# Eight-product and seven-product units in the second SwiGLU: five of eight units in seven products, with two of the weight sums formed in HBM

## The chip, the cores and the metric

The kernel runs on one core of one Trainium2 chip. The metric is device time in microseconds (us) of one execution. TensorE (PE) multiplies, VectorE (DVE) and ScalarE (ACT) work on vectors, GpSimd (POOL) and SyncE (SP) here mostly start DMA transfers. The kernel before took 1850.46 us in the median of three runs (1849.84 to 1851.51).

## The reference

One residual block on 16 meta tokens and 256 tokens of width 2048, all in float32:

```python
h = h + 0.5 * swiglu(rmsnorm(h, ffn1_norm), ffn1_w_gate, ffn1_w_up, ffn1_w_down)
u = rmsnorm(h, mix_norm);  z = u @ w_in
# z -> pooling channels | q | k | v | forget logits: pooled means and causal attention
h = h + mix @ w_out
h = h + 0.5 * swiglu(rmsnorm(h, ffn2_norm), ffn2_w_gate, ffn2_w_up, ffn2_w_down)
return h[:, N_META:]
# swiglu(x, wg, wu, wd) = (silu(x @ wg) * (x @ wu)) @ wd;  D_FF = 5632
```

Nearly all of the time goes into streaming 330 MB of weights through matrix products: the first SwiGLU, the input projection and attention, the output projection, and the second SwiGLU, in that order.

## The kernel before, in words

**Split products.** A float32 operand is split into a rounded part `hi` (ScalarE, L199) and a remainder `lo` (VectorE, L201), and a product is three matmuls: hi*hi, hi*lo, lo*hi. Each weight load `raw` is [128 x 1024] floats (512 KB), goes into one of six `raw` buffers, and is split into one of four `hi` and four `lo` buffers.

**One list for the whole kernel.** `W(...)` and `C(...)` append weight steps and other steps to `items`; `run` (L212 on) walks the list. It issues loads ahead (`do_dma`), splits up to `ahead` steps ahead, and lets `fn` multiply. All loads go through SyncE's queue, one after the other. The compiler's scheduler then orders the instructions of each engine, and may put one that waits for nothing ahead of others that were written earlier.

**First SwiGLU** (about 44 to 760 us). Every 512 KB load feeds 24 matmuls of 272 columns.

**Second SwiGLU** (from about 1124 us). It is tiled in 17 groups: 11 gate-up groups `f2_j` and 6 down groups `d2_tm` (thirds of 4, 4 and 3 gate-up groups, two halves each). A group runs over units (8 each; the last two down groups have 6), and a unit is a 2x2 block product. Kind "P" does it in eight products: two weight loads, two splits, 24 matmuls of 512 columns. Kind "S" does it in seven (Strassen-like): 21 matmuls, with four weight steps, since sums of weight blocks are operands too. `kinds` (L717) picks units 2, 4 and 6 as S, the last one always P. `PLAN` (L847) says which operand each product takes, and at which of the steps.

**An S unit before.** Step 0 splits only one half of the first load (512 columns, L886 to L890). Step 1 splits the second load; VectorE forms `T0` with two adds of 512 (L901, L902). Step 2 splits `T0`, and VectorE forms `T1` with two more adds (L907, L908). Step 3 splits `T1`. So VectorE does, per S unit, one half split, three whole splits and four half adds; per P unit two whole splits. The activation side (`operands`, L720) builds four sums per S unit and two per P unit, once for each unit.

**Around the groups.** `evac` functions combine the seven accumulators in PSUM on VectorE and ScalarE; `tokens_off` (L1027) transposes the gate-up results and calls `operands`, within units 2 and 3 of the next group.

GpSimd does nothing between its start and 805 us; then it clears two tiles and issues 20 small transfers for attention (L415, L466).

Of the kernel before, what the change touches and what calls it, by code (L numbers as in the profile page):

```python
# [8 lines left out]
F32 = mybir.dt.float32  # L9
# [3 lines left out]
ALU = mybir.AluOpType  # L13
# [22 lines left out]
def hymba_block(ctx: ExitStack, tc: tile.TileContext, t, out: bass.AP):  # L36
# [11 lines left out]
    lop = ctx.enter_context(tc.tile_pool(name="lop", bufs=4))  # L48
    hsp = ctx.enter_context(tc.tile_pool(name="hsp", bufs=1, side="right"))
# [106 lines left out]

    def W(src, nk, fn, split=None, ahead=2):
        items.append(("w", src, nk, fn, split or split_w, ahead))
# [53 lines left out]
    def run(items):  # L212
# [9 lines left out]
        def do_dma():  # L222
            n = st["d"]
            _, src, nk, _, _, _ = items[ws[n]]
            if n % 4 == 0 and n < 4 * len(FIRST):
                load_h(*FIRST[n // 4])
# [12 lines left out]
        for kind, _, _, fn, _, ahead in items:  # L239
# [5 lines left out]
            while st["s"] < min(n + 1 + ahead, len(ws)):  # L245
                do_split()
# [470 lines left out]
    def kinds(n):  # L717
        return ["S" if i in (2, 4, 6) and i < n - 1 else "P" for i in range(n)]
# [65 lines left out]
    def out_evac(d):  # L784
        def f():
# [6 lines left out]
            else:  # L792
                sq = x3p.tile([P, SEQ], F32, tag="sq2", name=f"sq_n2{d}")
# [36 lines left out]
    def finish2():  # L830

        f2 = later_pools["f2"]
        v, y, s = (f2.tile([P, 2], F32, tag=f"n{i}", name=f"n2_{i}") for i in range(3))
# [18 lines left out]
    def halfcols(x):  # L852
        return x.rearrange("p a n -> p (a n)").rearrange("p (m c) -> p m c", m=2)

    def group(name, side, src, evac, between):
# [23 lines left out]
        for u, kd in enumerate(units):  # L879
            raw = {}  # L880

            def first_block(r, n, raw=raw):
                raw[0] = halfcols(r)
# [3 lines left out]
                nc.scalar.copy(hi[:, 0], raw[0][:, 0])  # L887
                nc.vector.tensor_tensor(
                    out=lo[:, 0], in0=raw[0][:, 0], in1=hi[:, 0].bitcast(F32), op=ALU.subtract
                )  # L890
                return hi, lo

            def sums(r, n, raw=raw, i=0):

                def tile_(k):
                    return later_pools["f2"].tile([P, HALF, P], F32, tag=f"T{k}", name=f"{name}T{k}_{n}")
                if i == 0:
                    raw[1] = halfcols(r)
                    raw["T0"] = tile_(0)
                    T = halfcols(raw["T0"])  # L900
                    nc.vector.tensor_add(T[:, 0], raw[0][:, 0], raw[0][:, 1])  # L901
                    nc.vector.tensor_add(T[:, 1], raw[0][:, 1], raw[1][:, 1])  # L902
                    return split_w(r, n)
                if i == 1:
                    raw["T1"] = tile_(1)
# [230 lines left out]
```

## Time and profile before

| | |
|---|---|
| median of three runs | 1850.46 us (1849.84 to 1851.51) |
| profiled execution | 1850.18 us |
| its span, first to last instruction | 1848.4 us |
| TensorE busy | 1839.9 us, 11,718 matmuls |
| VectorE busy | 1348.7 us, 73% of the span |
| ScalarE busy | 969.5 us, 52% |
| DMA | 335.56 MB, mean 182 GB/s |
| mean granted TensorE clock | 1.000 |

The profile is one execution. Busy time of TensorE is the union of its matmul rows, which overlap: a matmul row of 512 columns lasts some 396 ns, but the next starts earlier, so what a matmul costs is read from the distance of starts. The same is true, less strongly, of VectorE. The DMA share is the mean busy share of the core's 16 DMA engines. A wait is put down to what ended it last.

### The profile page before, as it was taken

To read this page: it belongs to the slowest core of one execution; us is meant where nothing else is said; L and a number is where in the kernel's file an instruction comes from. 1 tells how busy PE (TensorE), PEld (TensorE's weight loads), DVE (VectorE), ACT (ScalarE), POOL (GpSimd) and SP (SyncE) were. 2 spreads that over 40 slices of the span, in tenths; PEclk is the share of its full clock that TensorE was granted. 3 is DMA by queue.
4 is the path that set the end of the run, shared out by engine and by line. 5 is a ranking of instruction groups with operands and counts; after the bars stand their busy time and mean duration, and the time that the engine had idled before them with its cause. 6 is when DMAs were issued, how large, how long until landed. Compare 5 with 4: busy or idle time off the path is not lost.

```text
span 1848.4 us, 29522 instructions
## 1 busy us (share of the span) xinstructions
PE 1839.9 (100%) x11718; PEld 1679.0 (91%) x11718; DVE 1348.7 (73%) x1848; ACT 969.5 (52%) x1302; POOL 12.4 (1%) x32
## 2 busy tenths in 40 slices
PE   9999999999999999999999999999999999999998
PEld 8999999999999999999999988888888888888887
DVE  7655544555544555678777878888998999988988
ACT  7434333444334343577675566666655555555563
POOL 0000000000000000002000000000000000000000
PEclk9999999999999999999999999999999999999999
DMA  8555555555555554565445555555666555656654
GB/s 287 172 171 171 176 178 172 173 176 174 174 173 177 176 171 153 171 201 161 142 156 160 182 188 179 197 189 182 194 200 201 191 190 191 193 192 204 201 186 137
DMA packets 96825, 335.56 MB, mean 182 GB/s; under 512 B 11424, under 2 KB 13488, under 8 KB 96688
## 3 DMA queue, kind: packets, MB, share of 16 engines
q1 hardware_dynamic: 96048, 333.65, 55.1%
q8 instruction: 91, 1.49, 0.3%
q14 instruction: 46, 0.38, 0.1%
q0 software_dynamic: 640, 0.04, 0.0%
HBM read 331.51 MB, written 2.10 MB: 180 GB/s over the span
## 4 chain that ended last, share of the span: by engine, by line
PE 95%; DVE 2%; ACT 1%; issue 1%; DMA 0%; SPq 0%; ACTq 0%; DVEq 0%
PE f1d L170 5%; PE f1u L171 5%; PE f1g L171 5%; PE f1g L172 5%; PE f1d L172 5%; PE f1d L171 5%; PE f1g L170 5%; PE f1u L170 5%; PE f1u L172 5%; PE wo L176 3%; PE z L170 2%; PE z L172 2%; PE z L171 2%; PE wo L180 2%; PE z L176 1%; DVE lo L201 1%
## 5 line engine op out<-in xcount | busy, mean ns | idle before, releaser
L199 ACT CAST hi<-raw 128x1024 fp32r<-128x1024 f32 (+2 forms) x601 | 609.4, 1016 | 638.5 <-PE f1g L171 144.3
L201 DVE TENSOR_TENSOR lo<-raw,hi 128x1024 fp32r<-128x1024 f32 (+2 forms) x601 | 708.1, 1180 | 322.0 <-ACT hi L199 318.9
L170 PE MATMUL f1g<-x,hi 128*128 128x272 f32 x704 | 203.9, 290 | 1.7 <-ACT hi L199 1.7
L172 PE MATMUL f1g<-x,lo 128*128 128x272 f32 x704 | 203.9, 290 | 0.3 <-DVE lo L201 0.2
L171 PE MATMUL f1u<-x,hi 128*128 128x272 f32 x704 | 203.8, 289 | 0.0
L171 PE MATMUL f1g<-x,hi 128*128 128x272 f32 x704 | 203.7, 289 | 0.0
L172 PE MATMUL f1u<-x,lo 128*128 128x272 f32 x704 | 203.6, 289 | 0.0
L170 PE MATMUL f1u<-x,hi 128*128 128x272 f32 x704 | 203.5, 289 | 0.0
L172 PE MATMUL f1d<-f1s,lo 128*128 128x272 f32 x704 | 203.1, 289 | 0.0
L170 PE MATMUL f1d<-f1s,hi 128*128 128x272 f32 x704 | 203.1, 288 | 0.0
L171 PE MATMUL f1d<-f1s,hi 128*128 128x272 f32 x704 | 202.8, 288 | 0.0
L170 PEld LDWEIGHTS f1g<-x,hi 128*128 128x128 f32 x704 | 132.3, 188 | 2.6 <-ACT hi L199 2.4
L172 PEld LDWEIGHTS f1g<-x,lo 128*128 128x128 f32 x704 | 133.3, 189 | 0.8 <-DVE lo L201 0.7
L171 PEld LDWEIGHTS f1d<-f1s,hi 128*128 128x128 f32 x704 | 133.9, 190 | 0.0
L172 PEld LDWEIGHTS f1u<-x,lo 128*128 128x128 f32 x704 | 133.4, 189 | 0.0
L171 PEld LDWEIGHTS f1g<-x,hi 128*128 128x128 f32 x704 | 132.6, 188 | 0.0
L171 PEld LDWEIGHTS f1u<-x,hi 128*128 128x128 f32 x704 | 132.6, 188 | 0.0
L170 PEld LDWEIGHTS f1u<-x,hi 128*128 128x128 f32 x704 | 132.3, 188 | 0.0
L170 PEld LDWEIGHTS f1d<-f1s,hi 128*128 128x128 f32 x704 | 132.3, 188 | 0.0
L172 PEld LDWEIGHTS f1d<-f1s,lo 128*128 128x128 f32 x704 | 132.3, 188 | 0.0
L170 PE MATMUL z<-x,hi 128*128 128x272 f32 (+3 forms) x384 | 111.3, 290 | 0.0
L172 PE MATMUL z<-x,lo 128*128 128x272 f32 (+3 forms) x384 | 110.4, 287 | 0.1
(780 smaller groups left out, 3771.5 us busy)
## 6 DMA issues: line engine op xcount, KB each, us to landing
raw<-in_wgu SPq DMA_DIRECT2D x344, 512.0 KB, 3.5
raw<-in_wd SPq DMA_DIRECT2D x168, 512.0 KB, 3.4
raw<-in_win SPq DMA_DIRECT2D x66, 512.0 KB, 3.5
raw<-in_wout SPq DMA_DIRECT2D x32, 512.0 KB, 4.3
raw<-in_wd SPq DMA_DIRECT2D x16, 256.0 KB, 3.3
raw<-in_wgu SPq DMA_DIRECT2D x16, 128.0 KB, 3.3
raw<-in_wgu SPq DMA_DIRECT2D x8, 256.0 KB, 5.4
out<-h SPq DMA_DIRECT2D x8, 256.0 KB, 3.3
```

Source lines behind the costliest of these rows:

```text
L170: nc.tensor.matmul(ps[:, :n], wh, x[:, 0, :], start=first, stop=False)
L171: nc.tensor.matmul(ps[:, :n], wh, x[:, 1, :], start=False, stop=False)
L172: nc.tensor.matmul(ps[:, :n], wl, x[:, 0, :], start=False, stop=last)
L176: nc.tensor.matmul(ps.rearrange("p (a n) -> p a n", a=2), wh, x, start=first, stop=last)
L180: nc.tensor.matmul(ps[:, SEQ:], wl, x[:, 0, :], start=False, stop=False)
L199: nc.scalar.copy(hi, raw)
L201: nc.vector.tensor_tensor(out=lo, in0=raw, in1=hi.bitcast(F32), op=ALU.subtract)
```

## The change

`kinds` now makes units 2 to 6 seven-product units: five of eight instead of three (in the last two down groups, with 6 units, three instead of two). The former `T0` is no longer added up on VectorE. Instead, `add_up` makes a [128 x 1024] tile in HBM for each S unit: two plain transfers on SyncE's queue copy the same half of the first weight block into both halves of the tile, HBM to HBM, 256 KB each with rows of 2 KB; two transfers on GpSimd's queue then add the two other halves to it (`accum_op=ALU.add`), 256 KB each. Step 2 loads that tile like a weight. `T1` stays on VectorE, as one tile `T`. Step 0 loads only the half that it splits.

The jobs of `add_up` are collected in the list `ahead`; `do_dma` is written to take one off every ninth step from step 20 on. There are 81 S units in place of 49 (55 of gate-up, 26 of down), so 81 jobs: 162 copies and 162 accumulating transfers.

To make room in SBUF, the scratch `sq` of the output projection and the small tiles of `finish2` use the buffer `t2`, which `operands` uses too.

```diff
...
     rawp = ctx.enter_context(tc.tile_pool(name="rawp", bufs=6))
     hip = ctx.enter_context(tc.tile_pool(name="hip", bufs=4))
     lop = ctx.enter_context(tc.tile_pool(name="lop", bufs=4))
+    dram = ctx.enter_context(tc.tile_pool(name="dram", bufs=1, space=bass.MemoryType.DRAM))
     hsp = ctx.enter_context(tc.tile_pool(name="hsp", bufs=1, side="right"))
 
     first_x, first_g, first_t = (ctx.enter_context(ExitStack()) for _ in range(3))
...
 
 
     items = []
+
+
+    ahead, AHEAD_EVERY = [], 9
 
     def W(src, nk, fn, split=None, ahead=2):
         items.append(("w", src, nk, fn, split or split_w, ahead))
...
         def do_dma():
             n = st["d"]
             _, src, nk, _, _, _ = items[ws[n]]
+            if n >= 20 and n % AHEAD_EVERY == 0 and ahead:
+                ahead.pop(0)()
+            if callable(src):
+                src = src()
             if n % 4 == 0 and n < 4 * len(FIRST):
                 load_h(*FIRST[n // 4])
             if src is not None:
...
             st["s"] += 1
 
         n = 0
-        for kind, _, _, fn, _, ahead in items:
+        for kind, _, _, fn, _, more in items:
             while st["d"] < len(ws) and loads[st["d"]] - loads[n] <= DMA_AHEAD:
                 do_dma()
             if kind == "c":
                 fn()
                 continue
-            while st["s"] < min(n + 1 + ahead, len(ws)):
+            while st["s"] < min(n + 1 + more, len(ws)):
                 do_split()
             fn(splits.pop(n))
             n = min(n + 1, len(ws) - 1)
...
 
 
     def kinds(n):
-        return ["S" if i in (2, 4, 6) and i < n - 1 else "P" for i in range(n)]
+        return ["S" if i in (2, 3, 4, 5, 6) and i < n - 1 else "P" for i in range(n)]
 
     def operands(src, kind, base, ext, name):
 
...
                 f2n["acc"] = x3p.tile([P, SEQ], F32, tag="acc2", name="acc_n2")
                 nc.scalar.activation(f2n["acc"], h[d][:, META:], AF.Square)
             else:
-                sq = x3p.tile([P, SEQ], F32, tag="sq2", name=f"sq_n2{d}")
+                sq = x3p.tile([P, SEQ], F32, tag="t2", name=f"sq_n2{d}")
                 nc.scalar.activation(sq, h[d][:, META:], AF.Square)
                 nc.vector.tensor_add(f2n["acc"], f2n["acc"], sq)
             u = d // 2
...
 
     def finish2():
 
-        f2 = later_pools["f2"]
-        v, y, s = (f2.tile([P, 2], F32, tag=f"n{i}", name=f"n2_{i}") for i in range(3))
+        n2 = later_pools["x3p"].tile([P, 6], F32, tag="t2", name="n2_t")
+        v, y, s = (n2[:, 2 * i : 2 * i + 2] for i in range(3))
         for i in range(2):
             ps = ps_q(f"ps_n2{i}")[:, :2]
             nc.tensor.matmul(
...
     def halfcols(x):
         return x.rearrange("p a n -> p (a n)").rearrange("p (m c) -> p m c", m=2)
 
+    def add_up(name, b1, b2):
+
+        got = {}
+
+        def job():
+            x = got[0] = dram.tile([P, HALF, P], F32, tag=f"sum{name}", name=f"sum{name}")
+            for m in range(2):
+                nc.sync.dma_start(out=x[:, 4 * m : 4 * m + 4, :], in_=b1[:, 4:, :])
+            for m, b in enumerate((b1[:, :4, :], b2[:, 4:, :])):
+                nc.gpsimd.dma_start(out=x[:, 4 * m : 4 * m + 4, :], in_=b, accum_op=ALU.add)
+
+        ahead.append(job)
+        return lambda: got[0]
+
     def group(name, side, src, evac, between):
 
 
...
             raw = {}
 
             def first_block(r, n, raw=raw):
-                raw[0] = halfcols(r)
+                raw[0] = r
                 hi, lo = (
                     later_pools["f2"].tile([P, 1, NB], F32R, tag=f"b{i}", name=f"{name}b{i}_{n}") for i in range(2)
                 )
-                nc.scalar.copy(hi[:, 0], raw[0][:, 0])
-                nc.vector.tensor_tensor(
-                    out=lo[:, 0], in0=raw[0][:, 0], in1=hi[:, 0].bitcast(F32), op=ALU.subtract
-                )
+                r = r.rearrange("p a n -> p (a n)")
+                nc.scalar.copy(hi[:, 0], r)
+                nc.vector.tensor_tensor(out=lo[:, 0], in0=r, in1=hi[:, 0].bitcast(F32), op=ALU.subtract)
                 return hi, lo
 
-            def sums(r, n, raw=raw, i=0):
-
-                def tile_(k):
-                    return later_pools["f2"].tile([P, HALF, P], F32, tag=f"T{k}", name=f"{name}T{k}_{n}")
-                if i == 0:
-                    raw[1] = halfcols(r)
-                    raw["T0"] = tile_(0)
-                    T = halfcols(raw["T0"])
-                    nc.vector.tensor_add(T[:, 0], raw[0][:, 0], raw[0][:, 1])
-                    nc.vector.tensor_add(T[:, 1], raw[0][:, 1], raw[1][:, 1])
-                    return split_w(r, n)
-                if i == 1:
-                    raw["T1"] = tile_(1)
-                    T = halfcols(raw["T1"])
-                    nc.vector.tensor_add(T[:, 0], halfcols(raw["T0"])[:, 1], raw[0][:, 0])
-                    nc.vector.tensor_add(T[:, 1], T[:, 0], raw[1][:, 0])
-                    return split_w(raw["T0"], n)
-                return split_w(raw["T1"], n)
+            def second(r, n, raw=raw):
+                raw[1] = r
+                return split_w(r, n)
+
+            def third_(r, n, raw=raw):
+                raw["T"] = later_pools["f2"].tile([P, HALF, P], F32, tag="T", name=f"{name}T{n}")
+                T = raw["T"]
+                nc.vector.tensor_add(T[:, :4], r[:, 4:], raw[0])
+                nc.vector.tensor_add(T[:, 4:], T[:, :4], raw[1][:, :4])
+                return split_w(r, n)
+
+            def fourth(r, n, raw=raw):
+                return split_w(raw["T"], n)
 
             steps = range(2) if kd == "P" else range(4)
             for st in steps:
...
                     for n, pr in enumerate(PLAN[kd]):
                         if pr[2] == st:
                             product(u, n, hl)
-                split = None
-                if kd == "S":
-                    split = first_block if st == 0 else (
-                        lambda r, n, f=sums, i=st - 1: f(r, n, i=i)
-                    )
-                W(src(u, st) if st < 2 else None, HALF, mul, split, ahead=3)
+                if kd == "P":
+                    W(src(u, st), HALF, mul, None, ahead=3)
+                elif st == 0:
+                    W(src(u, 0)[:, :4, :], 4, mul, first_block, ahead=3)
+                elif st == 1:
+                    W(src(u, 1), HALF, mul, second, ahead=3)
+                elif st == 2:
+                    W(add_up(f"{name}_{u}", src(u, 0), src(u, 1)), HALF, mul, third_, ahead=3)
+                else:
+                    W(None, HALF, mul, fourth, ahead=3)
             for fn in between.get(u, ()):
                 C(fn)
 
```

What the scheduler makes of it is seen in the order of the instructions. The first place is SyncE's queue early in the first SwiGLU; `raw` are weight loads, `sumf2_1_2` is the sum tile for unit 2 of gate-up group 1. Before:

```order
L229 DMA raw36_846<-in_wgu1 128x1024
L229 DMA raw37_876<-in_wgu1 128x1024
L229 DMA raw38_917<-in_wgu1 128x1024
L229 DMA raw39_947<-in_wgu1 128x1024
L229 DMA raw40_977<-in_wgu1 128x1024
```

Now, at the same loads:

```order
L870 DMA sumf2_0_5_1458<-in_wgu2 128x512 x2
L237 DMA raw40_989<-in_wgu1 128x1024
L870 DMA sumf2_0_6_1755<-in_wgu2 128x512 x2
L237 DMA raw41_1019<-in_wgu1 128x1024
L870 DMA sumf2_1_2_2052<-in_wgu2 128x512 x2
L237 DMA raw42_1060<-in_wgu1 128x1024
L870 DMA sumf2_1_3_2349<-in_wgu2 128x512 x2
L237 DMA raw43_1090<-in_wgu1 128x1024
```

The copies do not stand at every ninth step. They wait for nothing, and stand between neighbouring loads: one or two after each load. The first two copies stand behind load 27, the next two behind load 36, and all 162 are issued before load 127 (of some 730); behind that there are none.

The second place is the end of the accumulating transfers on GpSimd's queue, and what follows (`d2_21` is the last group of all, `one2` and `nil` are the two tiles cleared for attention):

```order
L872 DMA sumd2_21_2_18225<-in_wd2 128x512 x2
L872 DMA sumd2_21_3_18364<-in_wd2 128x512 x2
L872 DMA sumd2_21_4_18505<-in_wd2 128x512 x2
L407 MEMSET one2_9352 128x272
L408 MEMSET nil_9353 128x272
L423 DMA cuq0_9543<-c0_9531 1x16x16
```

All 162 accumulating transfers stand in front of GpSimd's work for attention, which stood right behind its start-up before.

The third place is VectorE in a gate-up group, with two S units in a row now (`f2_5` is group 5; `f2_5b1` is the half split, `lo` a whole split, `f2_5T` an add of 512):

```order
L901 TENSOR_TENSOR f2_5T0_559_15704<-raw558_15625 128x512
L201 TENSOR_TENSOR lo555_15665<-f2_5T1_554_15627,hi555_15663 128x1024
L902 TENSOR_TENSOR f2_5T0_559_15704<-raw558_15625,raw559_15646 128x512
L907 TENSOR_TENSOR f2_5T1_560_15725<-f2_5T0_559_15704,raw558_15625 128x512
L201 TENSOR_TENSOR lo556_15674<-raw556_15555,hi556_15672 128x1024
L734 TENSOR_TENSOR sg1_15659<-ga1_15655 128x256
L725 TENSOR_TENSOR gb1_15653<-ga1_15655,gb1_15653 128x512
L888 TENSOR_TENSOR f2_5b1_558_15693<-raw558_15625,f2_5b0_558_15692 128x512
L201 TENSOR_TENSOR lo557_15684<-raw557_15589,hi557_15682 128x1024
L736 TENSOR_TENSOR ge1_15654<-sg1_15659,ge1_15654 128x256
L201 TENSOR_TENSOR lo559_15709<-raw559_15646,hi559_15707 128x1024
L908 TENSOR_TENSOR f2_5T1_560_15725<-f2_5T1_560_15725,raw559_15646 128x512
```

and now:

```order
L911 TENSOR_TENSOR f2_5b1_586_16121<-raw586_16057,f2_5b0_586_16120 128x512
L744 TENSOR_TENSOR ge1_16102<-sg1_16107,ge1_16102 128x256
L205 TENSOR_TENSOR lo585_16113<-f2_5T584_16081,hi585_16111 128x1024
L205 TENSOR_TENSOR lo587_16134<-raw587_16069,hi587_16132 128x1024
L921 TENSOR_TENSOR f2_5T588_16142<-raw588_16094,raw586_16057 128x512
L205 TENSOR_TENSOR lo588_16147<-raw588_16094,hi588_16145 128x1024
L922 TENSOR_TENSOR f2_5T588_16142<-f2_5T588_16142,raw587_16069 128x512
L911 TENSOR_TENSOR f2_5b1_590_16172<-raw590_16118,f2_5b0_590_16171 128x512
L205 TENSOR_TENSOR lo589_16159<-f2_5T588_16142,hi589_16157 128x1024
L205 TENSOR_TENSOR lo591_16185<-raw591_16130,hi591_16183 128x1024
L921 TENSOR_TENSOR f2_5T592_16193<-raw592_16155,raw590_16118 128x512
```

Of four adds per S unit two are left, and S units follow each other without a P unit between them.

## Rows read from the trace of the kernel before

**Rows 1.** Page, part 1: busy time, share of the span, instructions of two engines

```profile
PE 1839.9 (100%) x11718; PEld 1679.0 (91%) x11718; DVE 1348.7 (73%) x1848; ACT 969.5 (52%) x1302; POOL 12.4 (1%) x32
```

**Rows 2.** Page, part 2: granted clock and DMA share, in tenths, 40 slices

```profile
PEclk9999999999999999999999999999999999999999
DMA  8555555555555554565445555555666555656654
```

**Rows 3.** Page, part 4: the chain that ended last, by engine

```profile
PE 95%; DVE 2%; ACT 1%; issue 1%; DMA 0%; SPq 0%; ACTq 0%; DVEq 0%
```

**Rows 4.** Stages: busy time (and instructions) of each engine, clock, DMA share, GB/s

```profile
core 0: us, PE busy (x) PEld busy (x) DVE busy (x) ACT busy (x) POOL busy (x), PEclk, DMA share, GB/s
15.00:20.00 5.00, 4.07 (x31) 3.62 (x29) 3.78 (x11) 3.75 (x10) 0.00 (x0) 1.00 0.99 331
46.00:370.00 324.00, 324.00 (x2567) 324.00 (x2567) 173.69 (x211) 129.11 (x151) 0.00 (x0) 1.00 0.53 173
1124.00:1848.00 724.00, 719.71 (x3148) 580.46 (x3147) 649.94 (x814) 416.04 (x481) 0.00 (x0) 1.00 0.58 189
1430.90:1474.50 43.60, 43.60 (x193) 35.19 (x192) 39.45 (x50) 26.06 (x31) 0.00 (x0) 1.00 0.59 194
1345.30:1388.20 42.90, 42.90 (x184) 34.47 (x183) 38.39 (x47) 22.04 (x23) 0.00 (x0) 1.00 0.61 197
```

**Rows 5.** Waits of the SyncE DMA queue, 46 to 370 us: total, times, longest

```profile
SPq L229 <- DVE lo L201: 225.4, 86, 3.2
SPq L229 <- DVE f1s L114: 59.6, 20, 3.3
```

**Rows 6.** Timeline of TensorE, second SwiGLU: first and last of 122 rows

```profile
1139.82 0.40 PE L874 MATMUL f_0q<-lo,x3e 128*128 128x512 f32 x1
...
1168.05 0.40 PE L875 MATMUL f_0q<-hi,x3e 128*128 128x512 f32 x1
```

**Rows 7.** Timeline of VectorE, two half-unit adds and two splits

```profile
1188.61 0.69 DVE L901 TENSOR_TENSOR f_1T<-raw 128x512 f32<-128x512 f32 x1
1189.21 0.69 DVE L902 TENSOR_TENSOR f_1T<-raw,raw 128x512 f32<-128x512 f32 x1
...
1196.78 1.22 DVE L201 TENSOR_TENSOR lo<-raw,hi 128x1024 fp32r<-128x1024 f32 x1
1197.91 1.22 DVE L201 TENSOR_TENSOR lo<-f_1T,hi 128x1024 fp32r<-128x1024 f32 x1
```

**Rows 8.** VectorE by line, 1430.9 to 1474.5 us: busy, mean ns, idle before, releaser

```profile
L201 DVE TENSOR_TENSOR lo<-raw,hi 128x1024 fp32r<-128x1024 f32 x13 | 15.8, 1221 | 3.1 <-ACT hi L199 3.1
L201 DVE TENSOR_TENSOR lo<-f_5T,hi 128x1024 fp32r<-128x1024 f32 x6 | 7.3, 1220 | 1.0 <-ACT hi L199 1.0
```

**Rows 9.** Timeline of SyncE queue: 17 loads issued after the first 20

```profile
16.81 27.12 SPq L229 DMA_DIRECT2D raw<-in_wgu  x17
```

**Rows 10.** Groups by line, 46 to 370 us, VectorE: busy, mean ns, idle before

```profile
L201 DVE TENSOR_TENSOR lo<-raw,hi 128x1024 fp32r<-128x1024 f32 x107 | 131.2, 1226 | 105.8 <-ACT hi L199 105.4
```

**Rows 11.** DMA queues, 20 to 40 us: packets, MB, share of 16 engines

```profile
q1 hardware_dynamic: 2221, 7.03, 96.3%
```

**Rows 12.** DMA queues, 15 to 20 us

```profile
q1 hardware_dynamic: 728, 1.64, 97.6%
```

**Rows 13.** DMA queues, 46 to 370 us: packets, MB, share of 16 engines

```profile
q1 hardware_dynamic: 15338, 55.82, 52.3%
```

**Rows 14.** DMA queues and issues, whole span: count, KB each, us to landing

```profile
q0 software_dynamic: 640, 0.04, 0.0%
...
raw<-in_wd SPq DMA_DIRECT2D x16, 256.0 KB, 3.3
...
out<-h SPq DMA_DIRECT2D x8, 256.0 KB, 3.3
```

**Rows 15.** Timeline of GpSimd: start, length of two issues

```profile
805.83 0.33 POOL L399 MEMSET one<- 128x272 f32 x1 [803.61 <-DVE acc_nm L136]
...
843.13 1.15 POOL L466 DMA_DIRECT2D cuk<-c  x2
```


## The prediction

> **What bounds the kernel now.** Read first the busy shares: TensorE is busy through the whole span and VectorE for 73% of it [rows 1], at full clock (2.4 GHz) in every slice [rows 2]. The chain that ended last is TensorE to 95% [rows 3]. Stage by stage the same holds: in the first SwiGLU from 46 to 370 us TensorE is busy 324.00 of 324.00 us, in a gate-up group of the second 43.60 of 43.60 [rows 4]. So a matmul less is worth its distance to the next one, as long as nothing else falls behind. What stands nearest behind differs by stage. In the second SwiGLU it is VectorE: 39.45 us busy of 43.60 in that group. In the first it is the transfers: the DMA engines are busy 53% of the time with weight loads alone, and 60% of the second SwiGLU's time [rows 4]. Loads in the first stage are not late: SyncE's queue waits 285 of 324 us for a buffer that VectorE has yet to free [rows 5].
>
> **What the change removes.** A unit turned from eight products to seven has 3 matmuls of 512 columns less. They start (1168.05 - 1139.82) / 121 = 0.2333 us apart [rows 6]. Fifteen groups turn two units, the last two groups one: 32 units, 96 matmuls, 22.4 us, if TensorE stays the bound there.
>
> **What it does to VectorE.** A turned unit brings one whole and one half split more. Whole splits start 1.13 us apart, half-width operations 0.60 [rows 7]. Two units a group: 2 x 1.13 + 2 x 0.60 = 3.46 us. Adds fall from 3 x 4 to 5 x 2, so 2 x 0.60 = 1.2 us go. Net +2.3 us a group: 39.45 becomes 41.7 us, while TensorE's 43.60 falls to 43.60 - 6 x 0.2333 = 42.2. VectorE would be 99% busy. Its 19 whole splits of this group also sat 4.1 us idle for ScalarE's half of the split [rows 8]. If that idle time cannot be squeezed, a group takes 41.7 + 4.1 = 45.8 us, 2.2 longer than before; if it all can, 42.2. Over 17 groups the edit lies between -22.4 and +37 us. A down group has more room, 38.39 of 42.90 us [rows 4]. I take half of the gain, -11 us, nearer the good end, since TensorE waited for none of that idle time.
>
> **What it adds to the transfers.** Each of 81 S units needs two copies and two accumulating transfers of 256 KB (0.262 MB). What matters is when. The order of SyncE's queue shows the copies not at every ninth step, but behind nearly every load: 160 of them between load 36 and load 126. Load 36 is issued near 44 us: 17 loads after the first 20 take until 16.8 + 27.1 [rows 9]. From 46 to 370 us 107 loads were split [rows 10], so one load feeds TensorE for 324 / 107 = 3.03 us, and the 90 loads for 272.5 us. Within that time SyncE's queue must now move 90 x 0.524 = 47.2 MB of weights and 160 x 0.262 = 41.9 MB of copies; and GpSimd's, which waits only for the copy it adds to, 41.9 MB more.
>
> What can the engines do? From 20 to 40 us, the loads' first rush, the queue moved 7.03 MB in 20 us at 96.3%: 365 GB/s at full share [rows 11]. With rows of 2 KB mostly, from 15 to 20 us, 1.64 MB in 5 us at 97.6%: 336 GB/s [rows 12]. The stage's own 55.82 MB took 52.3% of 324 us [rows 13], 329 GB/s, so those rates are not modest. I use 365.
>
> - Copies alone: 89.1 MB / 365 = 244 us. That fits into 272.5.
> - With the accumulating transfers at the price of a copy: 131.0 / 365 = 359 us, 87 more than TensorE needs. That no transfer in the trace goes from HBM to HBM bounds little: a store of 256 KB lands after 3.3 us as a load of 256 KB does [rows 14].
> - No row shows an accumulating transfer. It has two things to fetch, the new block and the sum so far, for one that it writes. If the fetched bytes count, its 41.9 MB are 83.9: 173.0 / 365 = 474 us, 201 more.
> - At three passes (two fetched and one written, one after the other) 214.9 / 365 = 589 us, +316.
>
> Below, the bound is 0: the engines could have time for them that no row shows. I take the second of these prices, two fetches, +201 us, since the copy is the nearest row and the adding has twice its input. While that lasts the loads are late, because they stand behind copies in the same queue: TensorE waits at each load, some 2.2 us. What hid the loads, 285 us of waiting for a free buffer, is gone.
>
> The Trainium skill speaks against the change here: by its page "DMA: Bandwidth & Descriptors", section "Issuing engines are not separate DMA queues", transfers started by ScalarE, SyncE and GpSimd end up on the same 16 engines and interleave. Its "Rules for kernel authors" add that an accumulating transfer reads its destination and writes it later. By the two the sum is +201 and not 0; if they did not hold, the copies alone would fit. No row here shows it, as GpSimd's queue carried 0.04 MB.
>
> **What else moves.** The accumulating transfers stand ahead of GpSimd's work for attention, first due at 805 us [rows 15]. Done by about 46 + 474 = 520 us, they delay none of it; an issue cost GpSimd some 0.57 us (two in 1.15), so 162 take it under 100 us. The load of a sum waits for its two additions, and all loads queue behind it on SyncE; the first sum is wanted after 1124 us, 600 us later, so nothing. In the second SwiGLU a group loads 5 x 0.262 = 1.3 MB more in 42 us, on top of a 60% share: about 70%, hidden. The shared `t2` buffer adds waits between ScalarE and VectorE in the output projection, off TensorE's path: 0, at the worst 1 us in each of 8 units.
>
> **Sum**, against the profiled execution (1850.2 us, span 1848.4 and 1.8 around it, 0.3 under the median): 1850.2 + 201 - 11 = 2040 us.
>
> **Rivals.**
> 1. *An accumulating transfer costs what a copy costs.* For it: the engines' time in the rows goes with bytes moved. Against it: it has two inputs. 1850.2 + 87 - 11 = 1926 us.
> 2. *The additions take no time from the loads* (they run in time of the engines that SyncE's queue leaves, or GpSimd issues them slowly enough). SyncE's own 244 us fit into 272.5, so the first SwiGLU is as long as before, and the saving in the second is left: 1850.2 - 22 to 1850.2 - 11, 1828 to 1839 us. It decides as long as the additions take under 28 us of the engines' time within the stretch. Against it: even at a copy's price they need 115 us. A half form, the additions drawn out far beyond the stretch by GpSimd, takes part of the 87: 1845 to 1885 us.
> 3. *TensorE's clock falls in the waits.* Then each load's 3.03 us become 6.06 at 1.2 GHz, and 90 loads 545 us, +273, more than the transfers' 474: 1850.2 + 273 - 11 = 2112 us. Against it: from 15 to 20 us TensorE was busy only 4.07 of 5 us, waiting for loads, and the granted clock was 1.00 [rows 4]. The Trainium skill ("TensorE: Matmul & The Clock Gate", section "HAM oscillation — how this bites in real kernels") tells of matmul loops whose clock falls again in each wait for a load; no run here shows it.
> 4. *The additions are dearer than two fetches*: at three passes 1850.2 + 316 - 11 = 2155 us, or more.
>
> **Chances.** The forecast 0.42, its own range 1980 to 2100 (the 336 GB/s of short rows for all but the weights would make +231, and 400 GB/s +160; VectorE's bad end adds 48); rival 1 0.22; rival 2 0.10, its half form 0.06; rival 3 0.10; rival 4 0.10. A range of 1885 to 2160 leaves out rival 2 with its half form and about half of rival 4. Half of the half form would not be told from no change (0.2%, some 4 us, is about what a measurement can tell): same 0.03. Faster 0.10, slower 0.87.
>
> **What would show it.** Right: from about 46 us on, DMA share near 1.0, TensorE busy some 58% at an unchanged clock, with waits for ScalarE's and VectorE's splits, and those for a load that landed late; behind load 126 all as before, but some 200 us later. The second SwiGLU shows 42 to 43 us a group and VectorE above 95%. The packets of GpSimd's queue give the price of an addition: twice a copy's time for the forecast, once for rival 1. Wrong: a DMA share well below 1.0 between 46 and 370 us with TensorE fully busy (rival 2), or a granted clock below 1.0 there (rival 3). The step most likely to fail is the price of an addition; the next, that the copies keep so close to the loads when they run.

## The result, and the profile after

The changed kernel took 2037.18 us in the median (2033.68 to 2039.57, 4 runs) against 1850.99 us before (1849.84 to 1852.56): a ratio of 1.1004, 95% interval 1.0985 to 1.1023. It is slower by 186 us. The forecast was 2040 us.

The page of the changed kernel, parts 1 to 4: busy time, granted clock and DMA share in 40 slices, DMA queues, and the chain that ended last. These answer to [rows 1 to 3] and to the `q0` row of [rows 14].

```profile
PE 1904.1 (93%) x11622; PEld 1687.5 (83%) x11622; DVE 1381.3 (68%) x1892; ACT 1003.6 (49%) x1366; POOL 144.6 (7%) x194
...
PEclk9989979888999999999999999999999999999999
DMA  9999999999655555545544555566666666666665
...
q1 hardware_dynamic: 131040, 397.37, 58.4%
q0 software_dynamic: 23968, 42.51, 11.8%
...
PE 56%; DMA 22%; DVE 12%; issue 5%; ACT 4%; ACTq 0%; SPq 0%; DVEq 0%
```

TensorE is busy 93% instead of 100%. The loss sits in the second to tenth slices, some 50 to 500 us: there the DMA share is 9 in every slice and the granted clock falls to 7 to 9 tenths. The chain, 95% TensorE before, now goes through transfers for 22%; and GpSimd's queue (`q0`), empty before, holds the engines 11.8% of the span for 42.51 MB, where SyncE's (`q1`) takes 58.4% for 397.37 MB. Over the whole span the additions cost nearly twice as much per byte (1.9 times).

The stages, same columns as [rows 4] (the last row is gate-up group 5, the one of 1430.9 to 1474.5 us before):

```profile
core 0: us, PE busy (x) PEld busy (x) DVE busy (x) ACT busy (x) POOL busy (x), PEclk, DMA share, GB/s
46.00:100.00 54.00, 54.00 (x429) 54.00 (x428) 31.02 (x46) 22.13 (x31) 14.66 (x18) 1.00 1.06 292
100.00:200.00 100.00, 74.25 (x480) 67.98 (x478) 29.97 (x37) 22.80 (x28) 28.54 (x35) 0.91 1.07 294
200.00:300.00 100.00, 72.21 (x452) 67.26 (x453) 31.99 (x40) 24.44 (x31) 29.41 (x36) 0.86 1.08 293
300.00:400.00 100.00, 77.60 (x510) 71.62 (x509) 28.01 (x30) 20.69 (x20) 29.44 (x36) 0.91 1.08 290
400.00:500.00 100.00, 76.83 (x458) 71.79 (x458) 29.26 (x34) 22.23 (x24) 27.75 (x34) 0.83 1.06 289
500.00:600.00 100.00, 98.89 (x776) 98.45 (x777) 56.22 (x71) 43.31 (x53) 0.81 (x1) 1.00 0.62 196
1287.00:2037.40 750.40, 720.78 (x3050) 548.95 (x3048) 685.87 (x854) 451.45 (x545) 0.00 (x0) 1.00 0.64 211
1601.00:1646.70 45.70, 44.49 (x187) 33.14 (x186) 41.69 (x52) 28.21 (x35) 0.00 (x0) 1.00 0.66 215
```

From 46 to 100 us TensorE still has every load in time, at a DMA share of 1.06. From 100 to 500 us it is busy 72 to 78 of 100 us. By these rows it sat idle 99.1 us in the four stretches and 1.1 in the next. The first SwiGLU lost more than these 100.2 us, as shown below: the other 62.6 are matmuls that took longer, mostly at the lower clock. From 600 us on the first SwiGLU runs as before. The first matmul of the input projection starts at 975.4 us, before at 812.6: the first SwiGLU lost 162.8 us. The second SwiGLU starts at 1287.0 us (before 1124.3) and ends with the span: 750.4 us, before 724.1, so it lost 26.3 us. The two together are 189.1, and the spans differ by 2037.4 - 1848.4 = 189.0. VectorE is busy 41.69 of 45.70 us in the group.

Inside the crowded stretch, 100 to 480 us, the DMA queues (packets; MB; share of the 16 engines' time) and the rounding `hi<-raw` on ScalarE, the first engine behind a load (busy, mean ns, idle before it, and what ended that):

```profile
DMA packets 49721, 110.67 MB, mean 291 GB/s; under 512 B 5526, under 2 KB 5526, under 8 KB 49699
...
q1 hardware_dynamic: 30400, 75.23, 55.3%
q0 software_dynamic: 19299, 35.14, 51.7%
```

```profile
L203 ACT CAST hi<-raw 128x1024 fp32r<-128x1024 f32 x75 | 78.5, 1047 | 299.0 <-DMA raw<-in_wgu 141.2 <-DMA raw<-in_wd 109.3 <-PE f1g L176 14.0
```

A share of 51.7% of 380 us for 35.14 MB is 0.517 x 380 x 16 / 35.14 = 89.4 engine-us per MB for GpSimd's queue; SyncE's, loads and copies, 44.7. So an addition occupies the engines twice as long, byte for byte, as the loads and copies beside it. ScalarE sat idle 299 us, and a load that had not landed ended 250 of them. Before, such a load was never late. SyncE's queue, which before waited for buffers [rows 5], now waits mostly for its own earlier transfers (the two longest totals, and what is left of the waits for a buffer; same stretch):

```profile
SPq L870 <- DMA sumf<-in_wgu: 79.2, 65, 3.1
SPq L237 <- DMA raw<-in_wgu: 49.5, 26, 3.4
SPq L237 <- DVE lo L205: 1.5, 4, 0.4
```

### The profile page after: what moved, and what is told of

Read it like the earlier page. It is cut to its first block, busy times and chain, and to the rows that moved or that the text cites. A ratio compares the mean times of both kernels' runs of the same rounds, so it can differ in the third digit from the quotient of the medians.

```text
span 2037.4 us, 30288 instructions
## 1 busy us (share of the span) xinstructions
PE 1904.1 (93%) x11622; PEld 1687.5 (83%) x11622; DVE 1381.3 (68%) x1892; ACT 1003.6 (49%) x1366; POOL 144.6 (7%) x194
## 3 DMA queue, kind: packets, MB, share of 16 engines
q1 hardware_dynamic: 131040, 397.37, 58.4%
q0 software_dynamic: 23968, 42.51, 11.8%
HBM read 437.68 MB, written 87.03 MB: 258 GB/s over the span
## 4 chain that ended last, share of the span: by engine, by line
PE 56%; DMA 22%; DVE 12%; issue 5%; ACT 4%; ACTq 0%; SPq 0%; DVEq 0%
DMA raw<-in_wgu 8%; DMA sumf<-in_wgu 7%; DVE lo L205 6%; DMA sumd<-in_wd 4%; PE wo L180 3%; DMA raw<-in_wd 3%; PE f1d L174 3%; PE f1g L176 3%; PE f1d L176 3%; PE f1d L175 3%; ACT hi L203 3%; PE f1g L175 3%; PE f1g L174 3%; PE f1u L175 3%; PE f1u L174 3%
## 5 line engine op out<-in xcount | busy, mean ns | idle before, releaser
L205 DVE TENSOR_TENSOR lo<-raw,hi 128x1024 fp32r<-128x1024 f32 (+2 forms) x650 | 764.9, 1182 | 481.8 <-ACT hi L203 477.7
L203 ACT CAST hi<-raw 128x1024 fp32r<-128x1024 f32 (+2 forms) x650 | 649.2, 1016 | 735.3 <-DMA raw<-in_wgu 175.6
L174 PE MATMUL f1d<-f1s,hi 128*128 128x272 f32 x704 | 211.2, 300 | 27.0 <-ACT hi L203 18.7
L174 PE MATMUL f1g<-x,hi 128*128 128x272 f32 x704 | 209.8, 298 | 21.5 <-ACT hi L203 21.4
L174 PE MATMUL f1u<-x,hi 128*128 128x272 f32 x704 | 210.2, 299 | 16.8 <-ACT hi L203 16.8
L176 PE MATMUL f1d<-f1s,lo 128*128 128x272 f32 x704 | 212.3, 302 | 12.8 <-DVE lo L205 12.8
L176 PE MATMUL f1u<-x,lo 128*128 128x272 f32 x704 | 211.3, 300 | 11.1 <-DVE lo L205 11.1
L175 PE MATMUL f1d<-f1s,hi 128*128 128x272 f32 x704 | 209.4, 297 | 0.7 <-DVE f1s L115 0.7
L175 PE MATMUL f1u<-x,hi 128*128 128x272 f32 x704 | 208.8, 297 | 0.0
L175 PE MATMUL f1g<-x,hi 128*128 128x272 f32 x704 | 207.9, 295 | 0.0
L174 PEld LDWEIGHTS f1d<-f1s,hi 128*128 128x128 f32 x704 | 139.2, 198 | 29.9 <-ACT hi L203 21.7
L174 PEld LDWEIGHTS f1g<-x,hi 128*128 128x128 f32 x704 | 137.0, 195 | 25.7 <-ACT hi L203 25.6
L174 PEld LDWEIGHTS f1u<-x,hi 128*128 128x128 f32 x704 | 137.9, 196 | 19.8 <-ACT hi L203 19.8
L175 PEld LDWEIGHTS f1d<-f1s,hi 128*128 128x128 f32 x704 | 140.2, 199 | 1.0 <-DVE f1s L115 1.0
L175 PEld LDWEIGHTS f1u<-x,hi 128*128 128x128 f32 x704 | 138.1, 196 | 0.0
L175 PEld LDWEIGHTS f1g<-x,hi 128*128 128x128 f32 x704 | 137.2, 195 | 0.0
```

What stands on the lines that cost most here:

```text
L174: nc.tensor.matmul(ps[:, :n], wh, x[:, 0, :], start=first, stop=False)
L175: nc.tensor.matmul(ps[:, :n], wh, x[:, 1, :], start=False, stop=False)
L176: nc.tensor.matmul(ps[:, :n], wl, x[:, 0, :], start=False, stop=last)
L203: nc.scalar.copy(hi, raw)
L205: nc.vector.tensor_tensor(out=lo, in0=raw, in1=hi.bitcast(F32), op=ALU.subtract)
```

## The experiments

In the profiles that follow, the input projection's first matmul tells the length of the first SwiGLU (812.6 us before), and the second SwiGLU is timed from its own first matmul to the end of the span (724.1 us before).

**1. No sums.** Splits the loss into its two parts.

```diff
-W(add_up(f"{name}_{u}", src(u, 0), src(u, 1)), HALF, mul, third_, ahead=3)
+W(src(u, 1), HALF, mul, third_, ahead=3)
```

> Leaves out the sums in HBM: no copies, no additions; step 2 of a seven-product unit loads the second weight block where the sum stood, so every load, split and matmul is as in the changed kernel. Theory A (the loss has two parts: about 163 us where the copies and additions crowd the loads of the first SwiGLU, about 26 us in the second SwiGLU, where five seven-product units in a row make VectorE and ScalarE late): 1877 us, 1870 to 1885; the first matmul of the input projection at 812 us again instead of 975, the second SwiGLU 750 us long. Theory B (the 26 us come from the transfers too, as the sum tiles in HBM are slow to load or wait for their additions): 1828 to 1850 us, the second SwiGLU 702 to 724 us.

Measured: 1877.41 us, ratio 1.0144 (1.0127 to 1.0160). The input projection starts at 812.5 us. Most of the first SwiGLU and the whole second one, in the columns above:

```profile
46.00:360.00 314.00, 314.00 (x2488) 314.00 (x2487) 168.26 (x204) 124.65 (x147) 0.00 (x0) 1.00 0.50 173
1124.20:1875.20 751.00, 720.97 (x3050) 549.49 (x3048) 685.85 (x854) 451.53 (x545) 0.00 (x0) 1.00 0.63 211
```

The second SwiGLU takes 751.0 us without a single transfer in HBM, as it does with them (750.4). Theory B falls: its 26 us do not come from the transfers, and the other 160 (2037 - 1877) come from nothing but the transfers.

**2. Plain second transfers.** Is it the second fetch?

```diff
-nc.gpsimd.dma_start(out=x[:, 4 * m : 4 * m + 4, :], in_=b, accum_op=ALU.add)
+nc.gpsimd.dma_start(out=x[:, 4 * m : 4 * m + 4, :], in_=b)
```

> GpSimd's 162 transfers overwrite instead of adding (the sums are left out), everything else as in the changed kernel: the same number of transfers, bytes written and queue order. Theory A (an addition's packet of 2 KB holds a DMA engine 176 ns where a plain one takes 84, and the engines' time is what the first SwiGLU waits for): 160 x 8 packets on each engine x 92 ns = 118 us of engine time less, at a share of 1.07 about 110 us: 1927 us, 1910 to 1945. Theory C (what costs is the number of transfers and their place in the queues, not the second fetch): 2015 to 2040 us.

Measured: 1944.92 us, 1.0510 (1.0495 to 1.0526); the input projection starts at 881.6 us, 69 later than before and 94 sooner than with additions. Queues from 100 to 350 us, and the same stretch in the columns above:

```profile
q1 hardware_dynamic: 25265, 62.46, 68.7%
q0 software_dynamic: 9034, 29.61, 33.2%
```

```profile
100.00:350.00 250.00, 213.33 (x1557) 200.48 (x1556) 95.26 (x114) 71.94 (x81) 59.03 (x113) 0.99 1.02 369
```

GpSimd's queue now takes 0.332 x 250 x 16 / 29.61 = 44.9 engine-us per MB, as much as SyncE's 44.0. Half the price, and 94 of the 163 us are gone, at the upper edge of what theory A allowed; theory C falls. That the doubled price is a second fetch is argued and not seen: the page counts 437.68 MB read from HBM in this run and in the changed kernel alike, by the instructions' own account. The run also changes the packets: the plain transfers went in packets of 4 KB (159 ns) and not of 2 KB, which per byte is 5% in their favour. The stretch is still full (1.02), so bytes at the plain price already do not fit.

**3. Copies alone.**

```diff
-for m, b in enumerate((b1[:, :4, :], b2[:, 4:, :])):
-    nc.gpsimd.dma_start(out=x[:, 4 * m : 4 * m + 4, :], in_=b, accum_op=ALU.add)
```

> GpSimd's additions are left out; the 162 copies stay in SyncE's queue where they are. Theory A (engines' time): 90 loads of 8 packets at 159 ns and 160 copies of 8 at 84 ns are 222 us on each engine, under the 272 us that TensorE needs for these loads; the first SwiGLU is as long as before, and 1877 us are left, 1870 to 1895. Theory D (the copies delay the loads because they stand ahead of them in one queue and hold its places): TensorE still waits at each load, 1930 us or more.

Measured: 1877.03 us, 1.0141 (1.0126 to 1.0156), the same as with no copies at all.

```profile
46.00:320.00 274.00, 274.00 (x2172) 274.00 (x2171) 147.11 (x178) 108.76 (x127) 0.00 (x0) 1.00 0.96 326
```

TensorE is busy 274.00 of 274.00 us with the copies ahead of the loads as in the changed kernel. The share is 0.96: they only just fit. Theory D falls; a place behind copies in one queue costs nothing as long as the engines have time. (My 222 of 272 us, a share of 0.81, came from median packets and was too low.)

**4. The pacing as written.** Each job's copies are queued behind the load that stands before them in the written order.

```diff
-                ahead.pop(0)()
+                if st.get("load") is None:
+                    ahead.pop(0)()
+                else:
+                    with tc.issue_after(st["load"]):
+                        ahead.pop(0)()
...
-                nc.sync.dma_start(out=raw, in_=src)
+                st["load"] = nc.sync.dma_start(out=raw, in_=src).ins
```

> The whole computation, but each pair of copies is kept behind the weight load that stood before it in the written order, so one job comes at every ninth step up to the end of the second SwiGLU. Theory A: a job is 4.2 us of engine time (2 x 8 x 84 ns + 2 x 8 x 176 ns); in the first SwiGLU it comes every 27 us, on a share of 0.53, and hides; in the second every 16 us, on a share of 0.65, which makes 0.91 and hides mostly: 1877 to 1900 us. Theory E (a transfer in HBM costs the loads the same wherever it stands): 2000 to 2040 us.

Measured: 1880.63 us, 1.0162 (1.0147 to 1.0177). The whole computation, all 324 transfers, and 157 us less than the changed kernel.

```profile
46.00:360.00 314.00, 314.00 (x2488) 314.00 (x2487) 168.65 (x204) 125.00 (x147) 19.77 (x24) 1.00 0.70 214
1124.60:1877.80 753.20, 722.10 (x3050) 549.25 (x3048) 685.81 (x854) 453.07 (x545) 64.99 (x80) 1.00 0.85 266
```

The transfers are hidden at a share of 0.70 in the first SwiGLU and nearly so at 0.85 in the second (753.2 us; 751.0 without any). 157 us of the cost was only when they ran. The 26 us stay.

**5. The adds off the chain.** This and the next run leave the sums in HBM out, as the first did, and look at those 26 us.

```diff
+                raw["r"] = r
                 return split_w(r, n)
...
             def fourth(r, n, raw=raw):
-                return split_w(raw["T"], n)
+                return split_w(raw["r"], n)
...
```

> As the first experiment (the sums in HBM left out, five of eight units in seven products), but the last step splits the loaded tile instead of the tile T that VectorE adds up; the two adds are still done, and nobody reads them. VectorE's and ScalarE's work is the same. Theory F (the 26 us are the chain add on VectorE, rounding on ScalarE, remainder on VectorE, once in every unit, which makes a unit last longer than its matmuls): the chain is cut, 1850 - 22 = 1828 us to 1845. Theory G (VectorE has too much work in the five units, 26 of 25 us, whatever the order): no change, 1870 to 1880 us.

Measured: 1830.08 us, 0.9889 (0.9876 to 0.9903).

```profile
1126.60:1829.70 703.10, 695.30 (x3050) 558.67 (x3048) 679.31 (x854) 464.53 (x545) 0.00 (x0) 1.00 0.67 226
```

The second SwiGLU falls from 751.0 to 703.1 us, though VectorE's busy time stays (679.3 us, 685.9 in the first experiment). Theory G falls: with the same amount of work the time is gone. It was that the tile T had to go from VectorE to ScalarE and back inside a unit. VectorE in the changed kernel, between the remainders of T of units 5 and 6 of group 5 (start, length, line, out<-in, idle time before and who ended it):

```profile
1633.39 1.23 DVE L205 TENSOR_TENSOR lo<-f_5T,hi 128x1024 fp32r<-128x1024 f32 x1 [0.52 <-ACT hi L203]
1634.53 1.22 DVE L205 TENSOR_TENSOR lo<-raw,hi 128x1024 fp32r<-128x1024 f32 x1
1635.67 0.69 DVE L921 TENSOR_TENSOR f_5T<-raw,raw 128x512 f32<-128x512 f32 x1
1636.27 1.22 DVE L205 TENSOR_TENSOR lo<-raw,hi 128x1024 fp32r<-128x1024 f32 x1
1637.41 0.68 DVE L922 TENSOR_TENSOR f_5T<-f_5T,raw 128x512 f32<-128x512 f32 x1
1639.26 1.23 DVE L205 TENSOR_TENSOR lo<-f_5T,hi 128x1024 fp32r<-128x1024 f32 x1 [1.17 <-ACT hi L203]
```

L922 finishes T, and the next thing VectorE can do is the remainder of T, for which ScalarE must first round T. From L922's start at 1637.41 to the remainder at 1639.26 are 1.85 us, of which 1.17 are idle. These remainders start 1639.26 - 1633.39 = 5.87 us apart; 21 matmuls take 21 x 0.2333 = 4.9 us. The group's four such distances are 7.74, 7.43, 5.81 and 5.87 us; in the first two VectorE also does work on the activation side. So such a unit runs at VectorE's pace. VectorE's own work in one, three whole splits and three half-width operations, is 3 x 1.13 + 3 x 0.60 = 5.2 us at the distances of [rows 7], a little over the matmuls' 4.9 even without a wait: it has to catch up in the P units, and any wait takes from that. Over the second SwiGLU VectorE waits for ScalarE's roundings (total, times, longest; before, then the changed kernel):

```profile
DVE lo L201 <- ACT hi L199: 64.5, 80, 1.6
DVE lo L205 <- ACT hi L203: 49.2, 70, 1.2
```

The total is no larger than before; the room for it is smaller. Before, VectorE's 649.94 us of work left 74 of the stage's 724 us. In the some 702 us that the matmuls alone would take now (724.1 - 22.4), its 685.87 us of work would leave 16, too few for such waits. It sat idle 64.5 us, and the stage took 750.4.

**6. No adds at all.**

```diff
...
-raw["T"] = later_pools["f2"].tile([P, HALF, P], F32, tag="T", name=f"{name}T{n}")
-T = raw["T"]
-nc.vector.tensor_add(T[:, :4], r[:, 4:], raw[0])
-nc.vector.tensor_add(T[:, 4:], T[:, :4], raw[1][:, :4])
+raw["T"] = r
...
```

> As the first experiment, but the two adds on VectorE are left out as well, and the last step splits the loaded tile. VectorE has 10 x 0.60 = 6 us less to do in a group. Theories F and G both: the full saving of 96 matmuls, 1850 - 22 = 1828 us, 1826 to 1834. If it stays above 1845, neither holds, and the wait lies with the loads or the buffers.

Measured: 1821.33 us, 0.9841 (0.9828 to 0.9854), some 7 us better than both theories. The second SwiGLU takes 695.0 us, 29.1 less than before; 96 matmuls are 22.4. The kernel before would thus have lost some 7 us to the adds and their chain itself; its trace shows TensorE idle for 724.1 - 719.4 = 4.7 us there. The work of the adds is worth 703.1 - 695.0 = 8 us, the chain 48.

**7. Four of eight, a job every fifth load.** This and the runs that follow keep the edit of experiment 4, which is left out of their cuts.

```diff
-return ["S" if i in (2, 3, 4, 5, 6) and i < n - 1 else "P" for i in range(n)]
+return ["S" if i in (2, 3, 5, 6) and i < n - 1 else "P" for i in range(n)]
...
-ahead, AHEAD_EVERY = [], 9
+ahead, AHEAD_EVERY = [], 5
```

> The whole computation: units 2, 3, 5 and 6 in seven products (four of eight; two of six in the last two groups, as before the change), sums in HBM, and a job kept behind every fifth load, so that all are done within the first SwiGLU. 15 groups x 3 matmuls x 0.2333 = 10.5 us less than before on TensorE. VectorE: one whole and one half split more (1.7 us), 8 adds in place of 12 (2.4 us less), so less than before, and never more than two such units in a row. Transfers: 4.2 us of engine time per job every 15 us, 0.28 on a share of 0.53, hidden. Theory A: 1840 us, 1838 to 1845, faster than before. Rival: two such units in a row already make VectorE late, or the transfers at 0.81 delay loads: 1850 us or more.

Measured: 1838.32 us, 0.9933 (0.9919 to 0.9946), faster than before, with the whole computation.

**8. The adds on GpSimd** (five of eight, every fifth load).

```diff
...
-nc.vector.tensor_add(T[:, :4], r[:, 4:], raw[0])
-nc.vector.tensor_add(T[:, 4:], T[:, :4], raw[1][:, :4])
+nc.gpsimd.tensor_add(T[:, :4], r[:, 4:], raw[0])
+nc.gpsimd.tensor_add(T[:, 4:], T[:, :4], raw[1][:, :4])
```

> The whole computation, five of eight units, a job kept behind every fifth load, and the two adds of a unit on GpSimd, which is idle in the second SwiGLU, in place of VectorE. If GpSimd's adds are short enough (two in under 3 us) and do not slow VectorE, VectorE falls to 35.7 of 42.2 us in a group: 1828 to 1835 us. If they make VectorE slower or are long themselves, the chain is longer than before: 1880 us or more.

Measured: 1912.98 us, 1.0338 (1.0324 to 1.0352). A miss, by the second branch. GpSimd's first adds in one group, and VectorE's splits of loads in the second SwiGLU (busy, mean ns, idle before):

```profile
L925 POOL TENSOR_TENSOR d_00T<-raw,raw 128x512 f32<-128x512 f32 x5 | 11.9, 2379 | 30.4 <-DVE lo L205 18.1 <-DMA raw<-sumd 12.3
```

```profile
L205 DVE TENSOR_TENSOR lo<-raw,hi 128x1024 fp32r<-128x1024 f32 x262 | 366.4, 1404 | 26.7 <-ACT hi L203 26.2
```

An add takes GpSimd 2.38 us on average in the group shown, the largest such mean, and 1.81 us over all 162; VectorE 0.69. VectorE's splits grew from 1.22 to 1.40 us meanwhile. The chain got longer, and VectorE slower.

**9. The adds first** (five of eight, every fifth load).

```diff
...
-nc.vector.tensor_add(T[:, 4:], T[:, :4], raw[1][:, :4])
-return split_w(r, n)
+add = nc.vector.tensor_add(T[:, 4:], T[:, :4], raw[1][:, :4])
+with tc.issue_after(add.ins):
+    return split_w(r, n)
```

> The whole computation, five of eight units, a job kept behind every fifth load, and VectorE does both adds of a unit before it splits the loaded sum, so that ScalarE rounds T while VectorE makes that remainder. Nothing is less; only the chain add, rounding, remainder has no split in its middle. Theory F: VectorE's 1.2 us of waiting in each unit go, the second SwiGLU falls from 750 us towards the 703 us of the run with the adds off the chain: 1836 us, 1830 to 1855. Theory G (the amount of work): 1875 us or more.

Measured: 1849.83 us, 0.9999 (0.9990 to 1.0008): no change from before. VectorE, one unit:

```profile
1465.80 0.68 DVE L925 TENSOR_TENSOR f_5T<-raw,raw 128x512 f32<-128x512 f32 x1
1466.52 0.69 DVE L926 TENSOR_TENSOR f_5T<-f_5T,raw 128x512 f32<-128x512 f32 x1
1467.13 1.22 DVE L205 TENSOR_TENSOR lo<-raw,hi 128x1024 fp32r<-128x1024 f32 x1
1468.38 1.23 DVE L205 TENSOR_TENSOR lo<-f_5T,hi 128x1024 fp32r<-128x1024 f32 x1
```

The split of the sum (1467.13) now stands between the last add and the remainder of T and fills ScalarE's time: the 1.17 us of waiting are down to 0.1. The second SwiGLU:

```profile
DVE lo L205 <- ACT hi L203: 14.1, 27, 1.9
```

```profile
1130.20:1847.40 717.20, 697.47 (x3050) 558.21 (x3048) 690.36 (x854) 453.74 (x545) 9.50 (x12) 1.00 0.70 229
```

The waits of 49.2 us are down to 14.1, and the stage takes 717.2 us instead of 750.4, so the chain is most of the loss. VectorE is now busy 690.36 of 717.20 us, 96%: with most of the waits gone, its amount of work is what stands next. The stage is still 14 us above the 703.1 of the run without the chain, and another 5 us are lost between input projection and second SwiGLU (316.5 us, before 311.7). The expected 1836 was too low by both.

**10. Four of eight, adds first, every fourth load.** Experiment 7 with the order of experiment 9 and

```diff
-ahead, AHEAD_EVERY = [], 5
+ahead, AHEAD_EVERY = [], 4
```

> The whole computation, units 2, 3, 5 and 6 in seven products, adds first, and a job kept behind every fourth load, so that the last addition stands ahead of the attention stage on GpSimd and the transfers leave that stage alone. The run with every fifth load lost some 6 us between the start of the input projection and the second SwiGLU. Theory A: these come back, 1833 us, 1829 to 1838. Rival: at every fourth load the engines are too full (0.53 + 4.2 / 12.1 = 0.88) and the first SwiGLU gets longer by more: 1838 us or more.

Measured: 1835.41 us, 0.9918 (0.9905 to 0.9932), the best full version.

```profile
46.00:360.00 314.00, 314.00 (x2487) 313.92 (x2486) 168.55 (x205) 125.60 (x147) 44.50 (x54) 1.00 0.93 270
1126.40:1833.00 706.60, 701.90 (x3101) 571.11 (x3099) 641.90 (x780) 440.21 (x511) 0.00 (x0) 1.00 0.65 218
```

The first SwiGLU keeps TensorE fully busy at a DMA share of 0.93. From the input projection to the second SwiGLU it takes 1126.4 - 814.8 = 311.6 us, as before; experiment 7 took 316.3. The second SwiGLU is as long as in experiment 7 (706.6 us), so with two such units in a row the order of the adds is worth nothing; what this run gains is the 5 us.

These 5 us go with the place of the additions in GpSimd's queue, and not with their traffic. In experiment 4, 24 of them ran in that stage, which took 311.7 us. In experiment 7 GpSimd clears the tile `one` at 816.4 us, behind an addition that waited for its copy, here at 808.0 (the input projections start within 0.3 us of each other), and ScalarE waits for it (experiment 7):

```profile
ACT cuk L414 <- POOL one L411: 4.5, 1, 4.5
```

That this wait is the whole of the 5 us is read from the trace and was not tried by itself.

## Why the prediction was right, and which of its steps were not

- **The order of the queues: right.** The copies ran where the order put them, and the additions with them, the last issued at 500.1 us (forecast: done by 520). Experiment 4 is the proof that this is the cause.
- **The price of an addition: right.** 89.4 engine-us per MB against 44.7, the price worked out from two fetches. Experiment 2 shows rival 1's price: +69 us in the first SwiGLU where 87 were worked out. The two rules that the prediction took from the Trainium skill ("DMA: Bandwidth & Descriptors", sections "Issuing engines are not separate DMA queues" and "Rules for kernel authors") agree with the rows: with both queues full the share reads 1.07 and the loads are late, and the addition's price is what two fetches would cost.
- **The term of the crowded stretch: right in kind, 38 us too large** (163 for 201). The rate was mis-sized: in the stretch the engines moved 291 GB/s, and fetched 35.14 MB / 380 us = 92 GB/s more for the additions, 383 GB/s in my count and not 365. That makes 173.0 / 383 = 452 us, +179. Most of the other 16 would be the loads already ahead when the rush began: TensorE did not wait before 100 us. Five loads ahead are worth 5 x 3.03 = 15 us; that is worked out and was not tried.
- **The second SwiGLU: this step failed.** I put it at -11 us, taking half of the gain, and it was +26.3, inside the bounds given (-22.4 to +37). I had found the 4.1 us a group in which VectorE waits for ScalarE's half of the split, and argued that TensorE "waited for none of that idle time". With five units in a row it does: group 5 took 45.70 us, close to the 45.8 that I had worked out for idle time that cannot be squeezed, and VectorE was busy 91% of it and not above 95%. What I had left out is why that time is there: in each unit the chain add, rounding, remainder makes VectorE wait, and at 99% of TensorE's time it has no room to make up for it (experiments 5 and 9). The down groups lost less, which is why +26.3 and not +37 came out.
- **So the total is nearer than its terms.** +163 and +26 stand where +201 and -11 were forecast; the errors of -38 and +37 cancel, and 2040 against 2037 owes that to luck.
- **Rival 2** (the additions hidden) is what experiments 4 and 10 make of it by spreading them; in the order as compiled it did not happen.
- **Rival 3** (the clock) happened in part, and the sign "TensorE busy some 58% at an unchanged clock" was missed: it was busy 284.5 of 380 us, 75%, at a granted clock of 0.88. That clock was 0.83 to 0.91 in four stretches of 100 us, where TensorE waited some 25 us in each. At such a place the rows show both levels, matmuls of 272 columns 0.23 us apart at 1.2 GHz and then 0.12 at 2.4 GHz, TensorE having waited for loads before:

```profile
149.95 0.43 PE L176 MATMUL f1u<-x,lo 128*128 128x272 f32 x1
150.18 0.43 PE L174 MATMUL f1u<-x,hi 128*128 128x272 f32 x1
...
151.87 0.29 PE L174 MATMUL f1g<-x,hi 128*128 128x272 f32 x1
151.99 0.29 PE L175 MATMUL f1g<-x,hi 128*128 128x272 f32 x1
```

The slower matmuls are in the 62.6 us beyond TensorE's idle time; by my estimate from the distances of starts some 46 of them. They seem not to have decided the time: the engines of the transfers were full throughout, and SyncE's queue waited only 1.5 of the 380 us for a buffer, so TensorE did not hold the loads back. At full clock TensorE would then have waited longer instead. That the stretch would be as long is argued from this and was not run. The Trainium skill ("TensorE: Matmul & The Clock Gate", section "HAM oscillation — how this bites in real kernels") has the clock fall in waits for loads, and the rows agree (0.83 to 0.91); the price of 273 us, all matmuls at half rate, was not paid.
- **Hidden things:** GpSimd's issue of an addition took 0.81 us, not 0.57, and was hidden; GpSimd's attention work was not delayed, as the last addition was issued at 500.1 us; the loads of the sums were never late. The DMA share of the second SwiGLU came to 0.64 and not to 0.70; its 60% before had been read too high (0.58 in [rows 4]).

## What to carry to other kernels

A transfer that waits for nothing is issued when the compiled order lets it, not where the program writes it: read the queue's order, and tie such transfers to the loads that they should follow. An addition in HBM is cheap only in time that the transfer engines have to spare; price it at twice its bytes and spread it over the stages in which they idle (experiment 4: the same 324 transfers, 157 us less). When an engine's busy share is near full, ask next for the longest chain inside one unit of work, back and forth between engines: here re-ordering two adds and a split gave back 33 us of the second SwiGLU at an unchanged amount of work, and turning fewer units (four of eight, not next to each other by more than two) was better still, 1835 us against 1850, of which 5 us are the attention stage.

## What the runs showed of the hardware that I had not expected

- An accumulating transfer from HBM to HBM costs about twice as much per byte as the loads and copies beside it: 89.4 and 44.7 engine-us per MB; its 2 KB packets hold an engine some 176 ns in the median, plain ones 84.
- The 16 engines' share reads up to 1.08 when two queues are full, so rows of the two queues overlap a little; 291 GB/s landed in that state, against 369 GB/s with plain transfers (experiment 2, 100 to 350 us).
- A float32 add of 512 columns takes GpSimd 1.81 us in the mean of 162 (experiment 8), 2.6 times VectorE's 0.69, and with such adds beside them VectorE's splits, which have two inputs, are 15% longer (1.22 to 1.40 us).
- Copies in a load queue at a share of 0.96 cost TensorE nothing (experiment 3): it was busy 274.00 of 274.00 us.
